# The SwiGLU down product of a hybrid decoder step as 15 rounds in place of 18 block products

## The chip, the cores and the metric

One core of one Trainium2 chip. The metric is the device time of one execution in microseconds (us), the median of several runs. All data is fp32.

## The reference

One inference step of a two-layer decoder: an mLSTM layer and then a forgetting-attention layer, each followed by a SwiGLU feed-forward block. Two request groups, a prompt of 1024 tokens (with 16 meta tokens ahead of it) and 64 sampled tokens, go through the same weights, so the feed-forward blocks work on 1104 columns of tokens. Cut to what the change touches:

```python
D_MODEL = 1024
D_FF = 2816                      # 22 tiles of 128

def swiglu(xn, w_gu, w_d):
    gu = xn @ w_gu
    return (jax.nn.silu(gu[..., :D_FF]) * gu[..., D_FF:]) @ w_d

def run_trunk(h, ...):
    for l in range(DEPTH):       # DEPTH = 2
        ...                      # mixer of the layer, added to h
        h = h + swiglu(rmsnorm(h, prm['norm_ffn'][l]), prm['w_gate_up'][l], prm['w_down'][l])
        if l == N_A_LAYERS - 1:
            shared = shared_kv(h, ...)
    y = rmsnorm(h, prm['norm_final'])
```

The change concerns the last product, `(...) @ w_d`, here called the down product: a weight of 2816 x 1024 against a hidden activation h of 2816 x 1104 (features by tokens).

## The kernel before, in words

**Layout.** Activations lie feature by token: 128 features on the partitions, tokens along the free axis. The tokens are cut into three groups `t` of 336, 384 and 384 columns (`TS`, `size`, `SL` = 384). The residual stream is in three tiles `H[t]` of eight feature tiles each (named `vA` in layer 0 and `Ht` in layer 1), with a copy `hD` in DRAM. Every fp32 product is made as three fp32r matmuls: each operand is split in a high part (a cast on ScalarE, line 338) and a low part (a subtraction on VectorE, line 339), and high x high, high x low and low x high are added in PSUM (`mm3`, lines 264 to 268).

**Feed-forward block** (`ffn`, from line 1454). First the gate and up products, in units of one feature tile (`Unit`, line 1484, matmuls on line 1505), which already use a scheme with fewer block products; the results, the tiles of h, are stored to DRAM as `hT[t]`. The last unit's leftover products are in `tail`. Then the down product.

**Down product before** (lines 1596 to 1853). `seq` is a list of 66 steps: three token groups `t`, two halves `z` of the output columns (512 each), eleven pairs `c` of h's tiles. A step multiplies two row tiles of the weight (256 x 512, one load of 512 KB, `w_load`) with two tiles of h: 4 output tiles x 2 x 3 = 24 matmuls into four PSUM banks `acc[m]`. After the eleven steps of a `(t, z)` the banks are added to `H[t]` (`add`, line 1480). With h's tiles cut in three groups this is 18 block products. h is loaded from `hT` by GpSimd's queue (`h_load`, line 1612), two tiles at a time, and split when `z` is 0; for `z` = 1 the split parts of the same group are used again. Weights are loaded five steps ahead and split two steps ahead (`w_split`). The squares for the next norm are made by `each` (`add_sq`, line 401), the norm of a finished group by `after` (layer 0, `norm_x`) or the final norm and output rows by `end` (layer 1, `final`), a little per step.

**Order.** `manual_schedule` fixes the order of the named engines to the order in which the program issues instructions; in the down stage these are TensorE, VectorE and ScalarE, while GpSimd's and SyncE's orders are chosen by the scheduler. Elsewhere (the value and key projections of `phase_a` and `phase_b`) other sets of engines are fixed, or none. Tiles that share memory wait for each other through semaphores.

**Queues.** SyncE's queue carries nearly all weights and the stores of h; GpSimd's queue carries stores of intermediate results to DRAM (`qkD`, `kD`, `qD`, `hD`, value rows) and loads of h and of some intermediate results; ScalarE issues almost no DMA.

## Time and profile before

| | |
|---|---|
| runs | 2864.53, 2862.03, 2862.07 us; median 2862.07 |
| span of the profiled execution | 2855.2 us, first to last instruction; its own time is not listed apart, the median is 6.9 us above the span |
| mean granted TensorE clock | 0.998 |
| down stage of layer 0 | 1005.0 to 1271.4 us |
| down stage of layer 1 | 2572.1 to 2844.6 us |
| DMA, whole span | 400 MB, 140 GB/s on average |

The span is the time from the first to the last instruction. The stages were read from TensorE's time line: line 266 to 268 writing the tile `dps` is the down product. A stretch's row gives the busy time of TensorE (PE), its weight loads (PEld), VectorE (DVE), ScalarE (ACT) and GpSimd (POOL), each with the number of instructions, then the granted TensorE clock, the share of the 16 DMA engines' time and GB/s. SP is SyncE. A group's row gives the line, engine and operation, what it writes and reads, the count, busy us and mean ns of one, and after the bar the idle time of the engine before these instructions with what ended it.

### The profile page before, as it was taken

What the parts mean: (1) busy time and instruction counts of PE and PEld (TensorE: products, weight loads), DVE (VectorE), ACT (ScalarE), POOL (GpSimd) and SP (SyncE); (2) the same over time, 40 slices, a digit from 0 to 9 for tenths busy, and PEclk for the clock granted to TensorE, in tenths of its full rate; (3) what the DMA queues carried; (4) which work ended last, traced back from release to release, by engine and by line L of the source; (5) the groups of instructions that cost most, each with busy time, mean ns of one, the idle gap of its engine ahead of it and who ended that gap; (6) DMA issues with size and microseconds to landing.
All of it is one profiled execution on the core that took longest, in us unless ns stands there. A gap on an engine that the chain in (4) does not pass through costs nothing.

```text
span 2855.2 us, 53625 instructions
## 1 busy us (share of the span) xinstructions
PE 2790.4 (98%) x20485; PEld 2671.0 (94%) x20485; DVE 1724.8 (60%) x3478; ACT 1311.8 (46%) x2622; POOL 1018.3 (36%) x1495
## 2 busy tenths in 40 slices
PE   7999999999999999999999999999999999999999
PEld 7998989999999999999999888777999999999999
DVE  6044555887787755553355443777478777765553
ACT  6132464444444434443344544878244444443432
POOL 3022333075556311115352202554307656531210
PEclk9999999999999999999999999999999999999999
DMA  7057655132222275544443676442412222237652
GB/s 214 19 145 175 165 160 180 48 91 76 79 84 78 95 269 198 205 144 133 149 165 129 243 282 222 156 141 87 161 60 87 79 74 84 74 102 251 221 186 99
DMA packets 312444, 400.19 MB, mean 140 GB/s; under 512 B 28143, under 2 KB 235051, under 8 KB 311163
## 3 DMA queue, kind: packets, MB, share of 16 engines
q1 hardware_dynamic: 277234, 277.79, 30.7%
q0 software_dynamic: 33728, 118.38, 12.7%
q8 instruction: 161, 2.64, 0.4%
q10 hardware_dynamic: 1224, 0.60, 0.1%
q14 instruction: 97, 0.79, 0.1%
HBM read 299.92 MB, written 96.77 MB: 139 GB/s over the span
## 4 chain that ended last, share of the span: by engine, by line
PE 71%; DVE 9%; issue 4%; ACT 3%; DMA 2%; POOL 1%; DVEq 0%; ACTq 0%; SPq 0%; POOLq 0%
PE m L1505 24%; PE dps L266 6%; PE dps L268 6%; PE dps L267 6%; PE tmps L266 3%; PE tmps L268 3%; PE tmps L267 3%; PE sp L2597 2%; DVE slot L339 2%; PE pops L268 1%; PE pops L266 1%; PE pops L267 1%; PE op L2693 1%; PE bps L266 1%; DVE s L2606 1%
## 5 line engine op out<-in xcount | busy, mean ns | idle before, releaser
L339 DVE TENSOR_TENSOR slot<-slot,slot 128x1024 fp32r<-128x1024 f32 (+3 forms) x263 | 266.4, 1015 | 129.9 <-ACT slot L338 123.6
L338 ACT CAST slot<-slot 128x1024 fp32r<-128x1024 f32 (+3 forms) x263 | 206.8, 788 | 229.3 <-PE dps L267 91.3
L1505 PE MATMUL m<-x1h,slot 128*128 128x384 f32 x640 | 178.0, 338 | 2.4 <-DVE vA L1480 0.8
L1505 PE MATMUL m<-x0h,slot 128*128 128x336 f32 x640 | 167.0, 316 | 0.0
L413 POOL TENSOR_TENSOR ns<-ns,nq 128x384 f32<-128x384 f32 (+1 forms) x59 | 63.9, 1083 | 208.8 <-ACT nq L411 207.6
L1505 PE MATMUL m<-x2h,slot 128*128 128x384 f32 x480 | 135.8, 337 | 0.0
L1612 POOL DMA_DIRECT2D hr<-hT x60 | 32.6, 543 | 283.1 <-DVE T_2l L339 69.6
L108 POOL TENSOR_TENSOR slot<-Ht 128x256 f32<-128x256 f32 x80 | 74.9, 946 | 151.3 <-DMA Ht<-in_w_gate_up 147.0
L108 POOL TENSOR_TENSOR slot<-vA 128x256 f32<-128x256 f32 x80 | 74.2, 937 | 151.5 <-DMA vA<-in_w_gate_up 147.8
L339 DVE TENSOR_TENSOR slot<-Ht,slot 128x256 fp32r<-128x256 f32 (+3 forms) x101 | 84.8, 841 | 63.7 <-ACT slot L338 63.7
L339 DVE TENSOR_TENSOR slot<-vA,slot 128x256 fp32r<-128x256 f32 (+3 forms) x101 | 85.7, 850 | 61.7 <-ACT slot L338 61.7
L1505 PEld LDWEIGHTS m<-x1h,slot 128*128 128x128 f32 x640 | 117.1, 188 | 3.4 <-DVE vA L1480 1.2
L1505 PEld LDWEIGHTS m<-x0h,slot 128*128 128x128 f32 x640 | 113.3, 188 | 0.0
L1505 PE MATMUL m<-x1l,slot 128*128 128x384 f32 x320 | 107.8, 337 | 0.0
L1505 PE MATMUL m<-x0l,slot 128*128 128x336 f32 x320 | 101.0, 316 | 0.0
L1505 PE MATMUL m<-T_2h,slot 128*128 128x384 f32 x320 | 97.1, 344 | 3.0 <-ACT Ht L1511 0.9
L2629 ACT ACTIVATE s<-s,nb 128x272 f32<-128x272 f32 (+7 forms) x126 | 98.9, 787 | 0.2 <-POOL nb L2620 0.2
L1505 PE MATMUL m<-T_4h,slot 128*128 128x384 f32 x320 | 95.9, 340 | 0.0
L2664 ACT COPY th<-tp 128x768 f32<-128x768 f32 (+1 forms) x80 | 73.6, 921 | 46.4 <-PE tp L2656 25.9
L108 POOL TENSOR_TENSOR Ht<-Ht 128x512 f32<-128x512 f32 (+1 forms) x60 | 84.5, 1409 | 28.4 <-DVE wl1l L339 28.4
L108 POOL TENSOR_TENSOR vA<-vA 128x512 f32<-128x512 f32 (+1 forms) x60 | 84.5, 1409 | 27.5 <-DVE wl0l L339 27.5
L2029 DVE TENSOR_REDUCE ss<-sqb 128x4 f32<-128x256 f32 (+1 forms) x72 | 30.2, 419 | 101.3 <-ACT sqb L2028 100.4
(838 smaller groups left out, 10267.7 us busy)
## 6 DMA issues: line engine op xcount, KB each, us to landing
slot<-in_w_down SPq DMA_DIRECT2D x88, 512.0 KB, 4.4
wr<-in_w_down SPq DMA_DIRECT2D x42, 512.0 KB, 4.5
wraw<-in_w_in_a SPq DMA_DIRECT2D x40, 512.0 KB, 4.0
vA<-in_w_gate_up SPq DMA_DIRECT2D x40, 512.0 KB, 4.0
Ht<-in_w_gate_up SPq DMA_DIRECT2D x40, 512.0 KB, 4.1
hr<-hT POOLq DMA_DIRECT2D x46, 384.0 KB, 5.2
kp<-in_cache_k SPq DMA_DIRECT2D x32, 512.0 KB, 6.2
vp<-in_cache_v SPq DMA_DIRECT2D x32, 512.0 KB, 7.4
```

The costliest lines, as they stand in the source:

```text
L108: self.net.nc.gpsimd.tensor_tensor(out=o, in0=a, in1=b, op=op)
L266: mm(ps, sh, mh, start=first, stop=False)
L267: mm(ps, sh, ml, start=False, stop=False)
L268: mm(ps, sl, mh, start=False, stop=last)
L338: self.nc.scalar.copy(hi, src)
L339: self.nc.vector.tensor_tensor(out=lo, in0=src, in1=hi.bitcast(F32), op=ALU.subtract)
L413: (nc.vector if x >= late else nc.gpsimd).tensor_tensor(out=s, in0=s, in1=sq, op=ALU.add)
L1505: nc.tensor.matmul(u.b[b][:, :n], w[p][:, k], x[q][:, k], start=new and k == i == 0, stop=k == 1 and i == 2, skip_group_check=True)
L1612: nc.gpsimd.dma_start(hraw[j], hT[t][:, 2 * c : 2 * c + 2])
L2597: nc.tensor.matmul(ps[z][:, :n], a[r, qs], b[r, at : at + n], start=(y == 0), stop=(y == 2))
L2629: nc.scalar.activation(ss[z, u], ss[z, u], AF.Exp, bias=nb[:, z : z + 1], accum_out=sm[:, u, z : z + 1])
L2664: nc.scalar.copy(th.rearrange("p x z (u h q) -> p h (x z u) q", h=2, q=64)[:, :, :n], pt[:, :, :n])
```

## The change

**The scheme.** The weight is cut in 2 column halves x 3 groups of seven row tiles (blocks `(z, k)`), h in 3 groups of seven tiles x 3 token groups (blocks `(k, t)`), which makes 18 block products. A bilinear scheme with 15 products computes the same: each round `p` multiplies a sum or difference of weight blocks with a sum or difference of blocks of h (`TERMS`), and its result, with signs, belongs to one or several of the six outputs. The 22nd tile of h and of the weight is left out of the scheme and added to some rounds as an extra row tile (round 0 is such a tile alone). Rounds are chained in PSUM: `DOWN` says for each round its sign, which outputs `(z, t)` take the running sum with which sign when the round is done, and whether the next round starts a new sum.

**Weight sums.** Four rounds use plain weight blocks (`RAW`), two a difference that GpSimd makes from two loaded blocks (`SOURCE`, `w_sub`), nine a sum that lies ready in DRAM (`COMBINED`, tiles `comb`). These are made by `combine`: a copy within DRAM issued by ScalarE and an accumulating DMA issued by GpSimd for each, in six portions that `phase_a` issues for layer 0 (during the input and the value and query/key products) and `phase_b` for layer 1 (during the value and key/query products).

**Sums of h.** Blocks of h are loaded whole from `hT` (`h_run`) and stay on chip; GpSimd forms the sums for two tiles at a time four steps ahead (`x_sum`), and each step's sum is split on ScalarE and VectorE (`x_split`) two steps ahead. Late in the stage two blocks are overwritten with sums (`merge`).

**Steps.** 62 steps of one or two row tiles. Each round boundary adds or subtracts the banks to `H` (`evict`). The norms and squares follow as the groups are finished, in another order.

**Memory and order.** The buffers of the gate and up products and the weight slots (`cg`, `cw`) are freed at the start of the stage and a new pool takes their place; in layer 0 the slots are made anew after the stage. GpSimd and SyncE are now in program order in the last unit and in the stage, too.

```diff
+RAW = {1: (0, 0), 3: (0, 2), 5: (1, 0), 6: (1, 1)}
+SOURCE = {4: ((0, 1), (0, 2)), 15: ((1, 1), (1, 2))}
+COMBINED = ((2, (0, 0), (0, 1)), (11, (0, 2), (1, 2)), (12, (1, 0), (1, 2)), (7, (0, 1), (1, 1)), (9, (0, 2), (1, 1)),
+            (8, 2, (1, 1)), (13, 11, (1, 0)), (10, 8, (1, 0)), (14, 13, (0, 0)))
+TERMS = {1: (((0, 0), 1), ((0, 1), 1), ((1, 0), -1)), 2: (((1, 0), 1),), 3: (((1, 1), 1), ((2, 0), 1), ((2, 1), 1)),
...
+DOWN = ((12, 1, ((1, 0, 1), (1, 1, -1)), None, True), (14, 1, ((0, 1, 1),), None, False),
+        (1, -1, ((0, 0, -1),), (0, 0), False),
...
+        (4, 1, ((0, 2, 1),), None, True), (0, 1, ((0, 1, 1),), (0, 1), False),
+        (9, 1, ((0, 2, 1), (1, 1, 1)), None, True),
+        (15, 1, ((1, 1, -1),), None, True), (0, -1, ((1, 2, -1),), (1, 2), False),
+        (6, 1, ((1, 2, 1),), None, True), (7, -1, ((0, 2, -1),), (0, 2), False))
...
+        for p, s, ev, last, new in DOWN:
+            js = list(range(7)) if p else []
+            if last:
+                js.append(NF - 1)
+            parts = [js[:1]] * (len(js) % 2) + [js[x : x + 2] for x in range(len(js) % 2, len(js), 2)]
+            for x, ts in enumerate(parts):
+                n = size[0] if p in (1, 5) or p in (2, 12) and x else SL
+                steps.append((p, s, ts, last, n, new and x == 0, ev if x == len(parts) - 1 else None))
...
+        def w_sub(i):
+            if i in wother:
+                n = len(steps[i][2])
+                a, b = (t[:, :n] for t in (wraw[i], wother[i]))
+                nc.gpsimd.tensor_tensor(out=a, in0=a, in1=b, op=ALU.subtract)
+                place["raw"].append(wother.pop(i))
...
+            h_run((2, 0), fresh[0], 0, 1)
+            w_load(nc.gpsimd)
+            w_load(nc.gpsimd)
+            h_run((2, 0), None, 1, 3)
+            w_load(nc.gpsimd)
+            h_run((2, 0), None, 3, 6)
+            h_run((0, 1), long(x0[1]))
+            h_run((0, 0), long(x0[0]))
+            for y in range(2):
+                w_split(y)
+                x_split(y)
+            w_load()
+            w_load()
+            for _ in tail:
+                pass
+            h_run((2, 0), None, 6, 7)
+            h_load(0, 4, 8)
+            h_load(1, 4, 8)
+            h_run((1, 0), long(x2[0]))
...
+            def evict(ev):
+                for m in range(4):
+                    for z, t, f in ev:
+                        h = H[t][:, 4 * z + m]
+                        tt(out=h, in0=h, in1=acc[m][:, : size[t]], op=ALU.add if f > 0 else ALU.subtract)
...
+            for i, (p, s, ts, last, n, lead, ev) in enumerate(steps):
+                w, x = wpart[i], xpart[i]
                 for m in range(4):
                     if lead:
                         acc[m] = bank("dps", "d")
+                    for k in range(len(ts)):
+                        for q, (a, b) in enumerate(((0, 0), (0, 1), (1, 0))):
+                            c = SL if lead and k == q == 0 else n
+                            nc.tensor.matmul(acc[m][:, :c], w[a][:, k, m * P : m * P + P], x[b][:, k, :c],
+                                             start=lead and k == q == 0, stop=k == len(ts) - 1 and q == 2,
+                                             skip_group_check=True)
...
+                if ev and (len(ts) == 1 or i == len(steps) - 1):
+                    evict(ev)
+                x_split(i + 2)
                 w_split(i + 2)
+                x_sum(i + 4)
+                w_sub(i + 3)
+                while len(wraw) <= i + 5 and w_load():
+                    pass
+                if ev and len(ts) == 2 and i < len(steps) - 1:
+                    evict(ev)
...
+def combine(self, l):
+
+    nc, w = self.nc, self.I["w_down"][l]
+    comb = self.comb[l] = {}
+    for part in (COMBINED[:5], COMBINED[5:7], COMBINED[7:]):
+        for p, a, _ in part:
+            comb[p] = self.dram.tile([7 * P, 512], F32, name=f"wc{l}_{p}")
+            nc.scalar.dma_start(comb[p], half(w, *a) if isinstance(a, tuple) else comb[a])
+        yield
+        for p, _, b in part:
+            nc.gpsimd.dma_start(comb[p], half(w, *b), accum_op=ALU.add)
+        yield
```

A step's raw weights go into three buffers, and a step of rounds 4 and 15 takes two of them. The three loads ahead of the stage are on GpSimd's queue, all later weights on SyncE's. In layer 0's `phase_a` the six portions are issued at the sixth input tile, ahead of the second and third value products, and at the 5th, 10th and 15th of the query/key products; in `phase_b` ahead of the second value product and of the first, second, fourth, fifth and seventh of the eight key/query products.

More of the change, by code (lines that the diff above doesn't have):

```diff
@@ L834, in phase_a @@
                     next(prep, None)
+                if x in (4, 9, 14):
+                    next(sums, None)
         def og_evict(m, t, ps):
@@ L1453, in ffn @@
 @_add(Net)
-def ffn(self, H, flat, l, weights, order, mix, small, each, after, end, early=None):
+def ffn(self, H, flat, l, weights, order, mix, each, after, end, cw, cb=None, early=None):
     nc, I = self.nc, self.I
@@ L1801, in ffn @@
[L1801 to L1816 removed]
+            tail = u.tail()
@@ L1848, in ffn @@
+                for _ in range(2 if p in (6, 7) else 1):
+                    next(norms, None)
+                for _ in range(99 if i == len(steps) - 1 else 2):
+                    if pend:
+                        pend.pop(0)()
             if after:
-                end(fp, pp, after(2))
+                end(dp, pp, after(2))
             else:
```

327 lines of the change are left out of this document (194 added, 133 removed), and 7 rows, old and new, of tables (DOWN, TERMS).

## The prediction

> **What bounds the kernel now.** I read the page's busy shares first, then a table of stretches over the two Down stages, then the time line of TensorE inside them, and last the other engines and the DMA queues in the places where the change puts work.
>
> ```profile
> PE 2790.4 (98%) x20485; PEld 2671.0 (94%) x20485; DVE 1724.8 (60%) x3478; ACT 1311.8 (46%) x2622; POOL 1018.3 (36%) x1495
> 1005.00:1085.00 80.00, 80.00 (x519) 80.00 (x519) 37.71 (x41) 30.88 (x36) 11.78 (x16) 1.00 0.74 252
> 1178.00:1266.00 88.00, 88.00 (x505) 87.73 (x504) 52.74 (x66) 36.58 (x53) 10.51 (x15) 1.00 0.53 181
> 2575.00:2842.00 267.00, 267.00 (x1612) 266.77 (x1611) 128.18 (x134) 97.59 (x116) 35.30 (x45) 1.00 0.57 192
> ```
>
> The last three rows are stretches inside the Down stages: their length, then the busy time of TensorE, its weight loads, VectorE, ScalarE and GpSimd, then granted clock, DMA share and GB/s. TensorE is busy for the whole of each at clock 1.00. So here a matmul less is time less, as long as nothing new makes TensorE wait; the other engines work half the stage or less.
>
> **Price of a matmul.** Rows of TensorE's time line, 336 columns wide and then 384:
>
> ```profile
> 1005.00 0.31 PE L266 MATMUL dps<-x0h,slot 128*128 128x336 f32 x1
> ...
> 1013.48 0.32 PE L267 MATMUL dps<-x0l,slot 128*128 128x336 f32 x1
> 1269.00 0.33 PE L267 MATMUL dps<-T_1l,slot 128*128 128x384 f32 x1
> ...
> 1271.27 0.33 PE L268 MATMUL dps<-T_1h,slot 128*128 128x384 f32 x1
> ```
>
> The 0.31 to 0.33 us are latencies of pipelined matmuls; the price is the distance of starts. 55 steps in 8.48 us are 0.154 us at 336 columns; 13 in 2.27 us are 0.175 at 384 (0.174 over 56 others).
>
> **The matmuls.** Before: 66 steps of 24, 1584 a layer: 528 of 336 columns (81.3 us) and 1056 of 384 (183.7 us), 265.0 us. After, counted from the list of rounds: 105 row tiles of products (15 x 7) and 6 for the last tile of h, each 4 x 3 matmuls, 1332: 336 of 336 columns (51.7 us) and 996 of 384 (173.3 us), 225.0 us. That is 40.0 us a layer, **80 us in all**. A full step (two row tiles) stays 24 matmuls, 4.17 us.
>
> **The engines beside it.** Rows of the stage of layer 0, mean in ns last before the bar, and two GpSimd rows of other stages:
>
> ```profile
> L339 DVE TENSOR_TENSOR slot<-slot,slot 128x1024 fp32r<-128x1024 f32 x40 | 49.3, 1237 | 56.6 <-ACT slot L338 56.6
> L339 DVE TENSOR_TENSOR x2l<-hr,x2h 128x768 fp32r<-128x768 f32 x8 | 7.6, 952 | 0.2 <-ACT x2h L338 0.2
> L1480 DVE TENSOR_TENSOR vA<-vA,dps 128x384 f32<-128x384 f32 x12 | 6.7, 555 | 16.8 <-PE dps L268 16.8
> L338 ACT CAST slot<-slot 128x1024 fp32r<-128x1024 f32 x40 | 41.9, 1050 | 53.9 <-DMA slot<-in_w_down 30.6 <-PE dps L267 23.1
> L338 ACT CAST x2h<-hr 128x768 fp32r<-128x768 f32 x8 | 6.7, 833 | 0.8 <-DMA hr<-hT 0.6
> L108 POOL TENSOR_TENSOR vA<-vA 128x512 f32<-128x512 f32 x40 | 57.4, 1436 | 27.5 <-DVE wl0l L339 27.5
> L2056 POOL TENSOR_TENSOR raw<-raw,gk 128x768 f32<-128x768 f32 x12 | 22.8, 1903 | 42.1 <-PE btp L2040 26.7 <-ACT sqb L2028 15.2
> ```
>
> VectorE: 55.5 weight splits of 1.24 us, as many splits of h of 0.95 (before, h was split for one half of the columns only), 76 evictions of 0.55 in place of 24 (more, because each round goes to one or two sums and the chain goes on in the same bank), and about 20 us of norms as before: some 183 of 225 us. ScalarE: 55.5 x (1.05 + 0.83) and norms, about 130. GpSimd, new: 52 sums of h of 1.90 at most, 8 merges, differences of weights in two rounds (the two rows give 1.82 us more per 1000 columns, so 2.37 for 1024): 130 to 150 with its DMA issues. A three-term round asks 3.8 us of GpSimd per 4.17 us step. All fit, so I price them at nothing; TensorE covers them, and with two steps of lookahead a late one shows only if it stays late. Banks: eviction follows each quarter step, so a round that evicts to one place holds nothing up. Two rounds evict to two places just before a short step: 1.1 us a quarter against 0.52 of matmul, about 2 us each.
>
> **The new chain in rounds 4 and 15.** Their weights are a difference of two halves, loaded as a pair into three raw buffers. A step's second half can be loaded only when the subtraction before has freed its buffer.
>
> ```profile
> slot<-in_w_down SPq DMA_DIRECT2D x88, 512.0 KB, 4.4
> vA<-in_w_gate_up SPq DMA_DIRECT2D x40, 512.0 KB, 4.0
> vA<-hD POOLq DMA_DIRECT2D x4, 1536.0 KB, 9.5
> qk<-qkD POOLq DMA_DIRECT2D x8, 512.0 KB, 7.1
> q1 hardware_dynamic: 277234, 277.79, 30.7%
> q0 software_dynamic: 33728, 118.38, 12.7%
> ```
>
> Load 4.0 to 4.4 us and subtraction 2.4 make 6.4 to 6.8 us per step against 4.17, three times in a row, with one to two steps ahead as cover: followed step by step with the split (1.05 + 1.24) behind it, round 4 loses 2.3 to 3.4 us and round 15, behind two short steps and the double eviction, 4.5 to 5.4. Ends 0 (loads landing in 3 us) and 9 a layer; I take 7, **+14**, by the 4.0 row, since no h is being loaded by then.
>
> **Start of the stage.** h is no longer streamed: 4.9 MB of h and weights and 1.4 MB of residual go through GpSimd's queue at once, issued in order from about 7 us before the stage, as the last unit's tiles come free. q0's bytes over its share (118.38 MB in 12.7% of 2855 us) are 326 GB/s, q1's 317. Tile 20 of h lands about 10 us into the stage and the residual about 16; step 3 wants the first 8 us in, the first eviction wants the second at 13, and the next step waits for that eviction since the chain stays in its bank. Behind that wait on VectorE stand the splits two steps on. Ends 0 (before, the hand-over shows no gap) and 9 (1.5 MB landing alone in 9.5 us); I take 5 a layer, **+10**.
>
> A TensorE wait may cost more than itself:
>
> ```profile
> 218.32 0.21 PE L1214 MATMUL n0p<-ident,n 32*128 32x32 f32 x1 [1.51 <-DMA n<-in_state_n]
> 217.00:219.00 2.00, 0.68 (x11) 0.67 (x13) 0.21 (x1) 0.00 (x0) 0.29 (x1) 1.00 1.15 249
> 219.00:221.00 2.00, 2.00 (x19) 1.83 (x14) 0.00 (x0) 0.00 (x0) 0.00 (x0) 0.83 1.23 183
> 221.00:223.00 2.00, 2.00 (x8) 2.00 (x7) 0.00 (x0) 0.00 (x0) 0.00 (x0) 0.50 1.19 295
> ```
>
> After a wait of 1.5 us the granted clock is 0.83 and then 0.50 for 4 us in all, 1.3 us of work lost. It followed small matmuls, not dense ones, so I add nothing for it. The Trainium skill, TensorE: Matmul & The Clock Gate, section "HAM oscillation", puts the point at gaps above about 3.4 us; by that rule only the stage's first waits could matter, some 1.7 us each, an estimate, and the sum would be about 2820; the trace's drop came after a shorter gap, so no run here supports the threshold itself.
>
> **Hand-over to the next phase.** Layer 0's weight slots are now freed and made anew after the stage, on top of buffers that the first value products still use. The first loads and splits of the next projection may come late by a 4.1 us load; ends 0 and 8, **+3**. The tail (the last evictions, squares and rows out) keeps its form: 0, ends -2 and 2.
>
> **The sums of weights in DRAM.** A layer has 9 copies (issued by ScalarE) and 9 accumulations (GpSimd) of 1.835 MB. Issue costs 0.4 to 0.9 us each on idle parts of their engines. The transfers share the 16 DMA engines with all loads, and the accumulations stand in GpSimd's queue ahead of its stores and loads; ScalarE must wait for an accumulation before some copies, with its evictions behind that wait.
>
> ```profile
> 65.00:137.00 72.00, 72.00 (x622) 72.00 (x621) 4.90 (x4) 13.58 (x30) 0.00 (x0) 1.00 0.12 27
> 137.00:200.00 63.00, 60.19 (x375) 58.22 (x374) 30.32 (x61) 20.57 (x33) 14.35 (x26) 1.00 0.44 134
> 200.00:235.00 35.00, 31.09 (x203) 29.62 (x203) 10.28 (x24) 8.40 (x14) 15.74 (x25) 0.95 0.95 197
> 1380.00:1408.00 28.00, 28.00 (x246) 28.00 (x246) 13.07 (x30) 12.84 (x35) 10.33 (x15) 1.00 0.44 145
> 1395.77 0.61 POOL L2049 DMA_DIRECT2D kDh<-bhi  x1
> 1404.57 0.61 POOL L2049 DMA_DIRECT2D kDh<-bhi  x1
> ```
>
> Layer 0's first five lie beside 65 to 137 us, where DMA is at 0.12: free. Its last two accumulations fall near 200, where DMA is at 0.95 and the recurrence's loads (7.1 us each) use the same queue. Layer 1's lie beside 27 us projections at 0.3 to 0.5. No row shows a copy within DRAM or an accumulation: from q0's rate 5.6 us each (9 x 5.6 = 51 us a layer, hidden), three times that (17 us) if reading twice and writing once cost in turn. Ends 0 and 80; I take **+8**, near the low end, because the stretches are mostly half idle. The Trainium skill, DMA: Bandwidth & Descriptors, section "Anatomy of one DMA", gives 2.0 us plus bytes over 436,000 per us for this queue, which would make 6.2 us each, an estimate; it says nothing of accumulation there, and the sum stays.
>
> **Sum.** -80 + 14 + 10 + 3 + 8 = -45 against the profiled execution, whose span is 2855.2 us, 6.9 under the median of 2862.07 that I carry it to: **2817 us**.
>
> **Rivals.** (1) All cover holds: the waits shrink to a few us and the time is 2782 to 2797. For it: half-idle engines and DMA shares of 0.53 to 0.74. Against it: the load-subtract chain is longer than a step. (2) Slower, by one mechanism: the accumulations hold up GpSimd's queue. If one takes 17 us, layer 1's five are 85 us of queue, and the stores of kD, a pair each 9 us (the two rows above) from two buffers, wait behind them; ScalarE stops for a free buffer and TensorE behind it. Some 20 us for that part, 25 for each of the two later ones and 30 for layer 0's last: 100 in place of 8, 2909 us. It decides when the total passes 53 us, at about 11 us an accumulation. Against it: the first five have a whole projection before kD's first store. (3) VectorE becomes the bound: 183 of 225 us is 81%, and in the rounds with a norm a step asks 0.95 + 1.24 + 0.55 + 1.1 of 4.17. One step in three late by 1 us is 20 a layer: 2857. Against it: its waits today are for ScalarE, not on itself.
>
> **How the numbers follow.** Forecast 0.50 (2797 to 2840), all covered 0.25, VectorE 0.14 (2840 to 2862), slower 0.11. Three runs spread over 2.5 us, so 0.2% (5.7 us) is about what can be told from no change. Faster 0.50 + 0.25 + 0.12, same 0.02, slower 0.11. The range goes from the floor with every wait gone, 2784, to 2860.
>
> **What would show it.** Right: 1332 matmuls a Down stage in 230 to 245 us; TensorE waits for VectorE at the fourth and fifth step; ScalarE waits for GpSimd's subtraction in rounds 4 and 15; phases before unchanged within 8 us. Wrong: stages of 225 us (1), kD's stores landing late with ScalarE waiting for them (2), TensorE waiting for splits in most steps (3), or matmuls whose distance is no longer 0.174 us.

## The result, and the profile after

The changed kernel takes 3190.31 us (3187.41 to 3193.6, four runs) beside 2862.66 us for the kernel before (2862.03 to 2864.53). The ratio is 1.1147, with a 95% interval of 1.1131 to 1.1163. The prediction was 2817 us.

The page of the changed kernel, busy shares of the span and a few rows of the span in 40 slices of 79.7 us:

```profile
span 3188.7 us, 53051 instructions
PE 2776.9 (87%) x19981; PEld 2636.7 (83%) x19981; DVE 1905.4 (60%) x3647; ACT 1321.2 (41%) x2670; POOL 1291.6 (41%) x1602
PE   0222999989999999887899999999999999999987
PEclk9965999999999999998999999999999999999989
DMA  9999257563222222843444438654242222218443
```

TensorE has 504 matmul instructions less, as meant (20485 to 19981), and is busy 14 us less, but for 87% of a longer span, not 98%. Two places show in its row. In the first four slices, 0 to 319 us, it is nearly idle and the DMA row stands at 9: nothing of the change was meant to be there. And in the two Down stages (slices 16 to 19 and 36 to 39) 7s and 8s now stand, in the first stage throughout and in the second in its later half, where before the row had 9 throughout.

Stretches of the kernel before, then of the changed one (length, busy time of TensorE, its weight loads, VectorE, ScalarE and GpSimd, granted clock, DMA share, GB/s): the first 330 us, the Down stage of layer 0, and the 40 us behind it.

```profile
0.00:330.00 330.00, 305.85 (x2196) 289.33 (x2197) 146.08 (x350) 115.63 (x256) 80.15 (x151) 0.99 0.54 143
1005.00:1270.00 265.00, 265.00 (x1581) 264.55 (x1581) 144.34 (x174) 109.33 (x145) 35.92 (x50) 1.00 0.60 204
1271.00:1311.00 40.00, 39.78 (x330) 39.18 (x329) 17.65 (x29) 13.99 (x35) 27.11 (x107) 1.00 0.58 194
```

```profile
0.00:330.00 330.00, 70.22 (x410) 66.03 (x411) 42.89 (x120) 41.87 (x94) 47.73 (x82) 0.79 1.00 244
1270.00:1565.00 295.00, 248.91 (x1344) 238.96 (x1343) 235.09 (x244) 114.89 (x163) 166.45 (x92) 0.93 0.53 179
1564.00:1604.00 40.00, 29.74 (x223) 28.31 (x221) 18.62 (x30) 12.28 (x27) 21.93 (x99) 0.89 0.47 156
```

The difference of the two spans is 333.5 us. From the starts of the first and the last matmul of each Down stage:

| part | before | after | difference |
|---|---|---|---|
| up to the first Down matmul | 1005.0 | 1269.9 | +264.9 |
| Down stage, layer 0 | 266.3 | 294.1 | +27.8 |
| between the stages | 1300.8 | 1321.0 | +20.2 |
| Down stage, layer 1 | 272.4 | 291.6 | +19.2 |
| tail | 10.7 | 12.1 | +1.4 |

So there are two losses. Both Down stages got longer, though each has 252 matmuls less, and most of the loss lies in the first 330 us, long before the first of them.

**The first 330 us.** What ScalarE and TensorE waited for there in the changed kernel (us in all, times, longest):

```profile
ACT x2h L757 <- DMA wc<-in_w_down: 78.3, 2, 64.7
ACT x0h L757 <- DMA wc<-in_w_down: 75.7, 2, 54.4
ACT rb L722 <- DMA wc<-in_w_down: 25.0, 1, 25.0
PE hps L741 <- ACT hs L758: 169.4, 6, 62.2
```

`wc` are the sums of weights in DRAM. ScalarE's casts of x stand in its queue behind copies of `wc` that wait for an accumulation, and TensorE waits for those casts. The copies from w_down and the accumulations, summed up by line (duration of the issuing instruction in ns min/median/max, first and last start in us):

```profile
L2008 ACTq DMA_DIRECT2D wc<-in_w_down x10: 503/4234/17396, 5.5 to 184.9; - x10
L2011 POOL DMA_DIRECT2D wc<-in_w_down x18: 1202/1220/1439, 19.7 to 310.7; - x18
```

All ten copies from w_down, layer 1's too, are issued between 5.5 and 185 us, and all 18 accumulations between 20 and 311 us. The program writes layer 1's beside the cache phase, some 1500 us later. The order of these instructions is the scheduler's: nothing that the program computes has to be done before the copies. An issue also took up to 17.4 us of ScalarE itself.

**The Down stage.** Groups of VectorE's instructions in layer 0's stage of the changed kernel (busy us, mean ns, idle before):

```profile
L361 DVE TENSOR_TENSOR dn0wl<-dn0raw,dn0wh 128x1024 fp32r<-128x1024 f32 x48 | 79.8, 1662 | 9.9 <-ACT dn0wh L360 9.2
L361 DVE TENSOR_TENSOR dn0xl<-dn0tmp,dn0xh 128x768 fp32r<-128x768 f32 x13 | 18.3, 1408 | 7.9 <-ACT dn0xh L360 7.9
L1939 DVE TENSOR_TENSOR vA<-vA,dps 128x384 f32<-128x384 f32 x52 | 25.4, 546 | 0.0
```

The split of 1024 columns took 1237 ns before and takes 1662; that of 768 columns 952 and now 1408. The eviction is as it was, 555 and 546. A stretch of VectorE's time line beside GpSimd's shows what decides:

```profile
1416.36 1.21 DVE L361 TENSOR_TENSOR dn0wl<-dn0raw,dn0wh 128x1024 fp32r<-128x1024 f32 x1
1417.49 2.59 DVE L361 TENSOR_TENSOR dn0xl<-dn0tmp,dn0xh 128x768 fp32r<-128x768 f32 x1
1420.01 2.86 DVE L361 TENSOR_TENSOR dn0wl<-dn0raw,dn0wh 128x1024 fp32r<-128x1024 f32 x1
1426.40 1.94 DVE L1939 TENSOR_TENSOR vA<-vA,dps 128x384 f32<-128x384 f32 x4
```

```profile
1415.14 0.90 POOL L665 DMA_DIRECT2D hD<-vA  x1
1416.52 2.75 POOL L1694 TENSOR_TENSOR dn0tmp<-hr,x0l 128x768 f32<-128x768 f32 x1 [0.48 <-DVE dn0xl L1713]
1419.35 2.44 POOL L1694 TENSOR_TENSOR dn0tmp<-dn0tmp,x1l 128x768 f32<-128x768 f32 x1
```

The split that starts in GpSimd's pause (1416.36) takes 1.21 us; the next ones, beside a sum of h, take 2.59 and 2.86, and the sum itself 2.75 in place of 1.90. Over the whole stage, the 18 splits of 1024 columns that lie beside no arithmetic of GpSimd take 1.22 us on average, and the 30 others 1.93. The eviction reads one operand in SBUF and one in PSUM and is not touched: 545 ns beside GpSimd's arithmetic and 546 without it. TensorE's waits in the stage, and one of them with the clock behind it:

```profile
PE dps L1957 <- DVE vA L1939: 29.1, 9, 6.9
PE dps L1957 <- DVE dn0wl L361: 9.1, 10, 2.3
PE dps L1957 <- ACT dn0wh L360: 5.8, 2, 4.7
1502.21 0.66 PE L1957 MATMUL dps<-dn0xh,dn0wh 128*128 128x384 f32 x1 [6.93 <-DVE vA L1939]
1504.00:1506.00 2.00, 2.00 (x8) 2.00 (x7) 1.86 (x3) 0.92 (x1) 2.00 (x2) 0.50 0.03 9
1508.00:1510.00 2.00, 2.00 (x13) 2.00 (x12) 0.68 (x1) 0.00 (x0) 0.88 (x1) 1.00 0.78 250
```

The 294 us are 225 of matmuls, 46 in which TensorE is idle, and the rest a slower clock: 0.93 over the stage, because it stands at 0.50 for some 3 to 6 us after most of the waits above 2 us.

### The profile page after: what moved, and what is told of

It reads as the page before. It is cut to its first block, busy times and chain, and to the rows that moved or that the text cites. A ratio compares the mean times of both kernels' runs of the same rounds, so it can differ in the third digit from the quotient of the medians.

```text
span 3188.7 us, 53051 instructions
## 1 busy us (share of the span) xinstructions
PE 2776.9 (87%) x19981; PEld 2636.7 (83%) x19981; DVE 1905.4 (60%) x3647; ACT 1321.2 (41%) x2670; POOL 1291.6 (41%) x1602
## 4 chain that ended last, share of the span: by engine, by line
PE 52%; DVE 13%; issue 6%; DMA 5%; ACT 4%; POOL 3%; ACTq 0%; DVEq 0%; SPq 0%; POOLq 0%
PE m L1536 20%; PE dps L1957 5%; PE tmps L287 3%; PE tmps L288 3%; PE tmps L286 3%; PE sp L2761 2%; PE op L2857 1%; DVE dn0wl L361 1%; DVE slot L361 1%; PE pops L286 1%; PE pops L287 1%; PE pops L288 1%; DVE dn1wl L361 1%; PE bps L286 1%; POOL dn1tmp L1694 1%
## 5 line engine op out<-in xcount | busy, mean ns | idle before, releaser
L1957 PE MATMUL dps<-dn0xh,dn0wh 128*128 128x384 f32 (+1 forms) x444 | 155.3, 350 | 36.1 <-DVE vA L1939 29.1
L1957 PE MATMUL dps<-dn1xh,dn1wh 128*128 128x384 f32 (+1 forms) x444 | 154.3, 347 | 26.3 <-DVE Ht L1939 20.1
L361 DVE TENSOR_TENSOR slot<-slot,slot 128x512 fp32r<-128x512 f32 (+3 forms) x175 | 155.0, 887 | 24.1 <-ACT slot L360 17.7
L1957 PE MATMUL dps<-dn0xh,dn0wl 128*128 128x384 f32 (+1 forms) x444 | 153.6, 346 | 9.1 <-DVE dn0wl L361 9.1
L1957 PE MATMUL dps<-dn1xh,dn1wl 128*128 128x384 f32 (+1 forms) x444 | 152.5, 344 | 4.8 <-DVE dn1wl L361 4.8
L1957 PE MATMUL dps<-dn0xl,dn0wh 128*128 128x384 f32 (+1 forms) x444 | 152.7, 344 | 0.9 <-DVE dn0xl L361 0.9
L1957 PE MATMUL dps<-dn1xl,dn1wh 128*128 128x384 f32 (+1 forms) x444 | 152.1, 343 | 0.6 <-DVE dn1xl L361 0.6
L360 ACT CAST slot<-slot 128x512 fp32r<-128x512 f32 (+3 forms) x175 | 114.5, 657 | 78.5 <-PE m L1536 67.5
L1957 PEld LDWEIGHTS dps<-dn0xh,dn0wh 128*128 128x128 f32 x444 | 88.3, 199 | 41.5 <-issue 28.8
L1957 PEld LDWEIGHTS dps<-dn1xh,dn1wh 128*128 128x128 f32 x444 | 87.9, 198 | 30.6 <-issue 18.3
## 6 DMA issues: line engine op xcount, KB each, us to landing
wc<-in_w_down POOLq DMA_DIRECT2D x18, 1792.0 KB, 34.2
```

Source lines behind the costliest of these rows:

```text
L360: self.nc.scalar.copy(hi, src)
L361: self.nc.vector.tensor_tensor(out=lo, in0=src, in1=hi.bitcast(F32), op=ALU.subtract)
L1957: nc.tensor.matmul(acc[m][:, :c], w[a][:, k, m * P : m * P + P], x[b][:, k, :c], start=lead and k == q == 0, stop=k == len(ts) - 1 and q == 2,
```

## The experiments

All are the changed kernel with the edit shown. Ratios are against the kernel before, run on the same chip. The experiments ran on several chips, on which the kernel before took 2861 to 2864 us, so differences of a few us between experiments are read from the ratios.

### e1: no sums of weights

```
-   nc.scalar.dma_start(comb[p], half(w, *a) ...)
-   nc.gpsimd.dma_start(comb[p], half(w, *b), accum_op=ALU.add)
-   get(w, 0, 0, js[0], len(js), 0, self.comb[l][p])
+   get(w, 0, 0, js[0], len(js))
```

> Leaves out the sums of weights in DRAM: no copies, no accumulations; the nine rounds that read a sum read the top left part of w_down in its place, the same bytes. Theory: the changed kernel lost its time in two places that have nothing to do with each other, some 265 us in the first 330 us of the span, where the copies and accumulations of both layers now stand, and some 55 us in the two Down stages. Then this kernel takes 2915 to 2935 us, the first 1000 us look as before the change, and the Down stages stay at about 300 and 290 us. Rival: the early loss comes from something else that the change moved (pools, order of loads): then about 3190 us again. Second rival: the stages are long because the loads of summed weights come late: then the stages shrink as well, to about 230 us each, and the time is near 2800 us.

2930.45 us, ratio 1.0233 (1.0215 to 1.0251). The first matmul of the first Down stage is at 1007.5 us, and the stages are 294.9 and 293.2 us long. The two losses are separate: 260 us for the sums, some 69 for the rest.

### e2: sums at the place where the program writes them

```
+   self.tc.keep_in_program_order(        # behind the instruction written before it on its engine
        nc.scalar.dma_start(comb[p], ...))
+   self.tc.keep_in_program_order(nc.gpsimd.dma_start(comb[p], half(w, *b), accum_op=ALU.add))
```

> All sums made, but each copy and accumulation is held in its engine's order behind the instruction written before it, so that they run where the program has them (layer 0: first projections, layer 1: projections of the cache phase). Theory: the loss of 265 us was the place and not the transfers; 10 to 40 us remain, for ScalarE's waits before the dependent copies and for DMA traffic: 2930 to 2970 us. Rival: the transfers cost their time wherever they stand (18 accumulations of 15 to 30 us each in GpSimd's queue): over 3050 us.

3110.6 us, ratio 1.0868 (1.0844 to 1.0893). The rival's side: only 80 of the 260 us come back. The DMA queues of this kernel (packets, MB, share of 16 engines):

```profile
q0 software_dynamic: 48768, 152.11, 17.4%
q10 hardware_dynamic: 10728, 33.64, 3.3%
```

The same without sums (e1):

```profile
q0 software_dynamic: 32352, 119.08, 12.2%
q10 hardware_dynamic: 1224, 0.60, 0.1%
```

The spans are 3108.1 and 2930.7 us. So the 18 accumulations take 183 us of all 16 engines, 10.2 us each, and the copies 5.5 each: 141 us a layer. At the written places that meets a DMA that is already half in use: the first 330 us of this kernel have a DMA share of 0.79 and 228 us of TensorE work in place of 304 in e1. The first Down matmul comes at 1105.5 us, 98 later than in e1. Layer 1's places cost nearly as much, 79 us more between the stages than in e1: there GpSimd's queue waits 40 us in all for accumulations ahead of other transfers, and ScalarE waits 32.9 us for the stores of kD, for which it does not wait at all in e1.

### e3: copies issued by GpSimd

```
-   nc.scalar.dma_start(comb[p], ...)
+   nc.gpsimd.dma_start(comb[p], ...)
```

> Copies issued by GpSimd in place of ScalarE, everything else as in the changed kernel: the order again puts them all early, but ScalarE's queue holds none. Theory: the loss at the start is ScalarE standing in order behind copies that it could not issue yet; without them most of 265 us comes back: 2930 to 3000 us. Rival: it is the DMA traffic, or GpSimd's queue with the stores and low parts behind the accumulations: 3100 us or more.

3172.38 us, ratio 1.1089 (1.106 to 1.1117): the rival again. ScalarE's queue holds no copy, yet nearly all of the loss stays. The first 330 us, and ScalarE's longest wait in them:

```profile
0.00:330.00 330.00, 96.80 (x586) 91.14 (x587) 50.63 (x125) 49.63 (x107) 59.42 (x100) 0.67 1.02 249
ACT hs L758 <- DMA hD<-hs: 148.5, 7, 28.5
```

The DMA engines are full (1.02). The start needs trips of blocks of x through DRAM (`hD`); their stores, which GpSimd issues, land 16 to 52 us after issue (median 40; 4.5 in e1), and ScalarE waits up to 28.5 us at a time. GpSimd itself waits 231 us in these 330 for transfers of the sums. The rival named DMA traffic and GpSimd's queue; this run does not part them, and whether the same wait would stand behind ScalarE's in the changed kernel is not shown.

### e5: sums in the gate and up stage

```
+   sums = self.combine(l)            # one copy or accumulation per next(), kept in program order
    for x in range(3, NF - 1):        # the 18 units of the gate and up stage
        ...
+           if g == 2:
+               next(sums)
```

> All sums of weights made, each layer's 9 copies and 9 accumulations one at a time, one per unit of the layer's own gate and up stage, in an order in which each finds its source long done. By the queue rows of the kernel with the sums at their written places, an accumulation takes 10.2 us of all 16 DMA engines and a copy 5.5, 141 us a layer; the gate and up stage has 450 us with a DMA share of 0.25. Theory: the sums cost what they take from a busy DMA and from queues behind them; here both are free, so the time is that of the kernel without sums plus 0 to 15 us: 2930 to 2945 us. Rival: ScalarE's issue of a copy (5 to 14 us in the two runs before) and GpSimd's issue stop the engines in any place: 18 x 5 us or more a layer on ScalarE, beyond 2980 us.

2931.22 us, ratio 1.0229 (1.0212 to 1.0246): as without sums, 259 us under the changed kernel. The stretch of 500 us ahead of the Down stage in the kernel before and here, and the copies:

```profile
500.00:1000.00 500.00, 494.20 (x2877) 488.90 (x2876) 391.42 (x590) 236.99 (x468) 251.26 (x248) 1.00 0.25 79
500.00:1000.00 500.00, 494.04 (x2874) 488.08 (x2873) 391.08 (x585) 235.71 (x466) 261.88 (x257) 1.00 0.53 141
L2007 ACTq DMA_DIRECT2D wc<-in_w_down x10: 497/507/592, 634.4 to 2578.4; - x10
```

The DMA share there goes from 0.25 to 0.53 and TensorE stays at 494 us. With one transfer on its way at a time an issue takes 0.51 us, not up to 17.4. The sums cost the DMA as much as in e2, but here they cost no time. This kernel does the whole computation and is what the change would have been with another place for its sums.

### e4 and e8: less of GpSimd's work

```
    # e4, on e1                                        # e8, on e4
-   if js and len(TERMS[p]) == 1 and len(js) == len(ts):    -   src = SOURCE.get(p)
+   if js and len(js) == len(ts):                           +   src = None
        return
```

> As the kernel without sums of weights, and GpSimd's sums of h are left out too: rounds of two and three terms split their first term alone (only the few steps with a row of the last tile of h keep theirs, with the merges and the differences of weights). VectorE's and ScalarE's work and all matmuls stay. Theory: the stages are long because VectorE's splits and GpSimd's sums slow each other: a weight split falls from 1.66 to under 1.35 us, the stages to 235 to 250 us, the time to 2800 to 2830 us. Rival: VectorE is late by its own load (evictions and splits in one queue): a split is still 1.6 us or the stages stay over 280 us, 2900 us or more. Between, some 2860 us: both.

> As the kernel without sums of weights and without GpSimd's sums of h, and rounds 4 and 15 load one half of w_down in place of two and leave out the difference. Theory: of the 54 us that the stage still is above its matmuls there, the load-and-subtract chain of rounds 4 and 15 carries 10 to 20 (four waits of 2 to 6 us around them), so 20 to 40 us less in all: 2870 to 2890 us. Rival (the term of the prediction, 7 us a layer, taken as an upper end with the cover of two steps): 2893 to 2905 us.

2907.7 us (1.0158, 1.0141 to 1.0175) and 2884.87 us (1.0075, 1.0058 to 1.0091). The splits fall to 1343 ns in e4, as expected, but the stages only to 282.6 and 278.9 us and the time to the rival's 2900 or more: the sums of h are 23 us of the loss, not 100. Each step showed something behind it. With GpSimd free sooner its loads of h and of the residual start sooner too, the burst of loads at the start of the stage gets denser (from 1035 to 1045 us the DMA share is 1.01, in e1 0.58), a weight load of round 1 comes late in it, and TensorE's wait there grows from 1.7 to 8.4 us (named after the eviction, which stands behind the split of that weight). e8 takes off another 23 us, in the range that the theory gave.

### e6: evictions ahead of the splits

```
-   if ev and (len(ts) == 1 or i == len(steps) - 1):
+   if ev:
        evict(ev)
    x_split(i + 2); w_split(i + 2); ...
-   if ev and len(ts) == 2 and i < len(steps) - 1:
-       evict(ev)
```

> The kernel without sums of weights, with one change in VectorE's order: at the end of every round the four evictions stand ahead of the splits for the step after the next, in place of behind them. Theory: the waits of 4 to 7 us at round ends (some 35 of the 48 us that TensorE waits in layer 0's Down stage) are evictions that stand behind a split which itself waits for a late sum of h; with the order turned most of them go, a part comes back as waits for splits before one-row steps: stages 270 to 280 us, 2885 to 2905 us in all. Rival: VectorE simply has too much to do, and the order moves the wait from one name to another: stages within 5 us of 296 and 293, 2920 to 2940 us, with TensorE's waits now for the splits.

2938.42 us, ratio 1.0259 (1.0242 to 1.0276). TensorE's waits in the stage of layer 0:

```profile
PE dps L1957 <- DVE dn0wl L361: 17.1, 15, 2.3
PE dps L1957 <- ACT dn0wh L360: 8.8, 6, 5.0
PE dps L1957 <- DVE vA L1939: 2.3, 3, 1.6
```

The wait for evictions falls from 29 to 2.3 us, and the others grow. The rival holds, though the stage of layer 1 grew by 6 us, to 299.6, where it had asked for at most 5: the name in the list of waits was that of the last in a late queue.

### e7: sums of h on VectorE

```
-   nc.gpsimd.tensor_tensor(out=o, in0=a, in1=runs[r][:, j, :n], ...)
+   nc.vector.tensor_tensor(out=o, in0=a, in1=runs[r][:, j, :n], ...)
```

> The kernel without sums of weights, with all 52 sums of h a layer made by VectorE in place of GpSimd. VectorE gets some 50 us more by its own durations (0.95 us for 768 columns). Theory: a GpSimd sum costs VectorE about as much as it saves (splits 1.66 instead of 1.24 us while both run), so that the move changes little: splits fall to 1.3 us, VectorE's busy time in the stage stays within 15 us, the time within 15 us of 2930. Rival: the two engines do not disturb each other and splits are long for another reason: VectorE's busy time grows by the full 50 us and the stage to over 320 us, 2980 us or more.

2940.64 us, ratio 1.0265 (1.0248 to 1.0282): by the ratios 9 us over e1, inside the theory's 15. Stretches of 280 us in the stage, without sums first and then with VectorE making the sums of h:

```profile
1010.00:1290.00 280.00, 234.76 (x1263) 224.83 (x1263) 222.04 (x226) 108.86 (x150) 160.74 (x90) 0.93 0.55 184
```

```profile
1010.00:1290.00 280.00, 230.70 (x1247) 222.67 (x1246) 217.95 (x277) 105.00 (x144) 53.02 (x37) 0.93 0.55 187
```

VectorE has 51 instructions more and is busy 4 us less, while GpSimd loses 108 us of work. By its price beside a quiet GpSimd (0.95 us) the 52 sums would have been some 50 us more. So a sum on GpSimd cost VectorE about all that it would have taken there itself.

### e9: the high part read from PSUM

On e5, two PSUM banks that stand free in the Down stage take a second copy of the high part:

```
+   nc.scalar.copy(hi[:, :n], wraw[i][:, :n])
+   for k in range(n):
+       b = bank("hp", "f")
+       nc.scalar.copy(b, hi[:, k].bitcast(F32))
+       tt(out=lo[:, k], in0=wraw[i][:, k], in1=b, op=ALU.subtract)
```

> The whole computation, with the sums of weights in the gate and up stage, and one change: ScalarE writes the high part of each weight piece a second time, into two PSUM banks that stand free in the Down stage, and VectorE takes the low part as SBUF piece minus PSUM piece, 512 columns at a time, so that it reads one SBUF operand and not two. Theory (the two engines disturb each other where both read two SBUF operands; evictions with one SBUF and one PSUM operand kept 546 ns all along): a 512-column split takes 0.65 to 0.7 us also while GpSimd works, GpSimd's 768-column sums fall from about 2.5 to about 2.0 us, the stages get 5 to 15 us shorter each, 2900 to 2920 us. Rival: the slowing does not depend on where the operands lie: two 512-column splits still take 1.7 us together, and ScalarE's extra 1.2 us a step make it 2930 to 2950 us.

2904.86 us, ratio 1.0139 (1.0122 to 1.0155), 26 us under e5, with no work left out. VectorE's splits and one of GpSimd's sums in the stage of layer 0:

```profile
L1678 DVE TENSOR_TENSOR dn0wl<-dn0raw,hp 128x512 fp32r<-128x512 f32 x108 | 69.7, 681 | 31.9 <-ACT hp L1677 31.0 <-issue 1.0
L1692 POOL TENSOR_TENSOR dn0tmp<-hr,x2l 128x768 f32<-128x768 f32 x3 | 5.5, 1842 | 6.8 <-DVE dn0xl L361 6.8
```

A split of 1024 columns, now two pieces, takes 2 x 681 ns beside a working GpSimd. The 108 pieces take 665 to 691 ns, though 65 of them lie beside arithmetic of GpSimd. This sum goes from 2762 ns in e5 to 1842; it moved the most, and the 27 sums of 768 columns go from 2391 to 1975 on average. Besides the place of one operand, the edit halves the split and gives ScalarE a second write. The halving is not what helps: in e10, beside a quiet GpSimd, a split of 512 columns from SBUF takes 690 ns and one of 1024 takes 1223. The Trainium skill, SBUF — State Buffer, section "Who interferes with whom", says that VectorE with two SBUF inputs contends with a GpSimd instruction that reads SBUF, and with at most one, outside its two-port modes, does not. By that rule the splits of h, left as they were, should stay slow: the trace agrees (13 of 768 columns at 1173 ns, 10 at 1392; the 20 beside arithmetic of GpSimd 1480 on average, the 15 others 946).

### e10 to e13: what is left

Each on e8. e10: squares on VectorE, no merges. e11: only the last eviction into each place. e12: both. e13: e12 without the residual's load.

```
    # e10                                       # e11
-   self.add_sq(H, t, m, sp, x, 4)              +   if gone.get((z, t), 0) + 1 < ...:   # not the last
+   self.add_sq(H, t, m, sp, x, 0)              +       continue
-   if p in (4, 9, 0) and merge and i > 40:         # e13
+   if False:                                   -   nc.gpsimd.dma_start(H[t][:, a:b], self.hD[...])
```

> As the kernel without sums of weights, sums of h and weight differences, and now GpSimd has next to no arithmetic in the Down stages: the sums of squares go to VectorE, the merges of runs are left out. Theory (what is left of the 47 us above the matmuls is still the two engines disturbing each other): splits at 1.24 us, stage of layer 0 under 260 us, 2855 to 2870 us. Rival (what is left is the burst of loads at the start and VectorE's own chain of evictions and splits): 2875 to 2890 us.

> As the kernel without sums of weights, sums of h and weight differences, with the evictions of a round left out unless they are the last into their place: 24 a layer as before the change, in place of 76; TensorE then goes from round to round without a wait for VectorE. Theory (evictions in the middle of a chain are what the rounds add to TensorE's path): some 15 us less a layer, from the waits named for evictions (8.6 us for the residual's load, and 1 to 3 us at five round ends), 2850 to 2860 us. Rival (splits and loads set the pace, the evictions only show where): 2875 to 2885 us.

> Both of the two before together: no arithmetic of GpSimd and 24 evictions a layer. If the causes named so far are all, the stage is its matmuls plus the burst of loads at the start (225 + 10 us), and the time 2835 to 2850 us, 10 to 25 us under the kernel before the change: the 20 us of the hand-over after layer 0 stay. Rival: a cause not named yet holds the stages at 250 us or more, 2865 us or more.

> As the kernel without GpSimd arithmetic and with 24 evictions a layer, and the residual (2 x 4.4 MB from DRAM, issued in the first 70 us of each stage) is not loaded: the evictions add to what stands in its place. Theory (the 28 us a layer that the stage there still is above its matmuls come mostly from the burst of h, residual and weights in its first 55 us, where the DMA share is 1.0 and the weight loads come late): 5 to 12 us less a layer, 2828 to 2842 us. Rival (the start is latency of the chain load, high part, low part, and not bytes): within 4 us of 2851.

e10 2864.93 us (1.0003, 0.9993 to 1.0012); e11 2859.32 (0.9985, 0.9975 to 0.9995); e12 2850.97 (0.9955, 0.9938 to 0.9972); e13 2834.94 (0.9902, 0.9885 to 0.9918). In e10 the split is at 1223 ns, its old price, and the stage of layer 0 at 262 us, a little over the theory's 260. e12 lies a little above the theory's band and keeps stages of 253 and 254 us, which the rival had asked for; e13 says what part of that is. Two stretches of 10 us, some 30 us into the stage, in e12 and then in e13:

```profile
1040.00:1050.00 10.00, 7.64 (x43) 6.73 (x41) 3.28 (x4) 3.42 (x4) 2.29 (x3) 1.00 1.03 397
1050.00:1060.00 10.00, 6.62 (x32) 6.07 (x33) 2.70 (x3) 1.71 (x2) 0.00 (x0) 0.85 1.02 418
```

```profile
1040.00:1050.00 10.00, 10.00 (x59) 10.00 (x59) 4.32 (x5) 3.94 (x5) 0.00 (x0) 1.00 1.02 420
1050.00:1060.00 10.00, 9.32 (x59) 8.87 (x58) 5.59 (x7) 4.36 (x5) 0.00 (x0) 1.00 0.69 261
```

With fewer bytes the burst at the start ends some 10 us sooner, the weights are there and TensorE is nearly full; the stages are 242 and 244 us. The first begins 4.3 us later, though, the part between them grows by 2.4, and the whole gain is 16 us. So of the 28 us above the matmuls, about 8 are bytes. What the rest is, the first chain of load, high part and low part or small waits, no run parts.

### e14 and e15: the work moved rather than left out

e14 is e9 with the squares on VectorE. e15 is e14 with the differences for rounds 4 and 15 made in the gate and up stage:

```
+   keep(nc.sync.dma_start(t[z], part(half(w, *b), z)))
+   keep(nc.scalar.activation(t[z], t[z], AF.Copy, scale=-1.0))
+   keep(nc.gpsimd.dma_start(part(d, z), t[z]))
    ...                                     # after the seven row tiles
+   keep(nc.gpsimd.dma_start(d, half(w, *a), accum_op=ALU.add))
```

> The whole computation: sums of weights in the gate and up stage, splits with the high part in PSUM, and the sums of squares in the Down stages on VectorE in place of GpSimd (18 additions a layer, 1.4 us on GpSimd, 0.56 on VectorE). Theory (GpSimd is the longer queue, its three-term sums are what the splits wait for): 5 to 12 us less than with the split from PSUM alone, 2893 to 2900 us. Rival (VectorE's own queue is what counts): 2903 to 2912 us.

> As the one with the squares on VectorE, and the differences of weights for rounds 4 and 15 are made in the gate and up stage too: ScalarE negates one half, 128 rows at a time, it is stored to DRAM and the other half accumulated onto it; rounds 4 and 15 then load one piece like the others. Theory (the load-and-subtract chain costs 11 us a layer, as the kernel without it showed): 18 to 26 us less, 2868 to 2880 us, still above the kernel before the change. Rival (what those rounds waited for was VectorE's backlog, or the extra work disturbs the gate and up stage): less than 8 us gained, 2888 us or more.

2901.94 us (1.0144, 1.0127 to 1.0161) and 2896.87 us (1.0119, 1.0102 to 1.0136). Both theories asked for more. By its ratio e14 gains nothing over e9 (1.0139), and e15 is 5 us under e14, as its rival had it. In e15 the stages fall from 277.1 and 277.8 to 268.0 and 262.5 us, the 24 us that the theory gave. But the first Down matmul comes 8.8 us later and the part between the stages grows by 12.8: most of what the load-and-subtract chain cost is paid again in the gate and up stage, where TensorE now waits for ScalarE's evictions. Ahead of the first Down stage of e15:

```profile
PE m L1529 <- ACT vA L1535: 9.1, 9, 5.3
```

In e14 that row is 1.6 us. e15 is the fastest changed kernel that does the whole computation, and it is still 1.2% above the kernel before; e12, which leaves out all this work, is only 0.45% below it. No version here that does the whole computation wins.

## Why the prediction was wrong, point by point

- **Matmuls, -80 us: right.** 1332 a layer (3 x 444 by line and tile), at 0.174 us where TensorE does not wait.
- **DRAM sums, +8 (ends 0 to 80): the step that failed, by 251 us.** Measured 259 (3190 against 2931 in e5). Two errors are in it. I took the sums to run where the program writes them, and the trace shows all of them issued in the first 311 us; that is worth 80 us (e2). And I priced an accumulation at 5.6 us, "hidden"; it takes 10.2 us of the whole DMA and the copy that I left out 5.5, so a layer needs 141 us of DMA and not 51. Between 65 and 137 us, where I had put five of nine, there was room for 63. The upper end of 80 was also too low for the written places, 180 us (e2 against e1). The issue price of 0.4 to 0.9 us held for ScalarE's copies only with one on its way (0.51 in e5); in the changed kernel the median is 4.2.
- **Other engines at nothing: the second step that failed.** I added up VectorE at 183 of 225 us by durations measured beside a quiet GpSimd (36 us of work in 265) and put 130 to 150 us on GpSimd beside it. The stage shows VectorE at 235 us and GpSimd at 166 of 295. The two prices were right each by itself and wrong together: in e10, with GpSimd at 17 us, VectorE is at 182, the forecast's figure.
- **A clock term of 0: wrong.** I added nothing, since the one drop in the trace of before followed small matmuls. Here the clock was 0.93 over the stage, some 20 us of 295. The Trainium skill, TensorE: Matmul & The Clock Gate, section "HAM oscillation", puts its point at gaps above 3.4 us, and that was nearer than my 0: in layer 0's stage a drop followed each of the five waits above 3.4 us. It is not borne out as a limit: in e9 a wait of 2.33 us was followed by matmuls at 0.50 for 3 us.
- **Rounds 4 and 15, +14:** 23 us when left out (e8), and 24 in the Down stages when moved (e15). The mechanism was right: ScalarE waits 20.8 us in layer 0's stage for the subtraction, the sign that was asked for. The size was too small, 7 a layer where leaving the chain out gives 11 to 12; why is not shown, since e8 takes away the second load as well as GpSimd's work.
- **Start of the stage, +10:** the place was right: waits of 4.7 and 1.7 us and a slow clock behind the first in layer 0. The first is the one forecast, though the list names the weights: ScalarE's cast of the last tiles of h waits 9.3 us for their load, which ends 13 us into the stage and not 10, and the cast of the weights stands behind it. No wait for the residual is seen there: the first evictions go straight after a split, and at the second wait VectorE goes without a pause from a split, slow beside GpSimd, to the eviction. Its bytes counted all the same once other work was gone: leaving its load out gave 16 us over both layers (e13).
- **Hand-over, +3:** measured 20.2. TensorE waits 5.9 us for the last norm and then 4.4 and 3.0 for the first weights in the remade slots; 29.74 us of work in 40 after the stage, at clock 0.89. I had priced one late load, and neither the norm nor the clock. VectorE's load in the stage is not the reason: e13, where it is busy 160 of 243 us, has the same 5.9.
- **Rivals.** The second (accumulations too dear, deciding at about 11 us each) named the right transfer. One takes 10.2 us of the DMA and lands 23.8 us after issue in e2, and its mechanism, GpSimd's queue held up and ScalarE waiting for the stores of kD, is seen there, at the written places. It had 100 us in all, where e2 shows 180, and nothing of the changed kernel's own order. The third (VectorE becomes the bound) named the right engine for the stage, at 20 us a layer where 70 stood above the matmuls. The first has its form in e12 and e13: with nearly all added work gone the time is 2851 and 2835, not 2782 to 2797. None had both losses at once.
- **What would show it.** The stages were to take 230 to 245 us; they take 294 and 292. The phases ahead were to stay within 8 us and grew by 265. Of the signs against the forecast "TensorE waiting for splits in most steps" came nearest: e6 shows 21 waits for the weights' splits in 62 steps, once the evictions are out of their way.

The two stages and the hand-over together are 67 us of loss for 80 us of matmuls saved: 147 us of new waits and slower clock. Left out one after another, sums of h give 23, differences 23, squares and merges 20, evictions 14 (26 without the step before), the residual's load 16. How much of that is the two engines in each other's way and how much is VectorE's own work is shown only in part: 26 us for the weight splits (e9). The splits of h were not tried with an operand in PSUM.

## What to carry to other kernels

An instruction that depends on nothing has no place in the program until something holds it there: look up where the scheduler puts it before pricing what covers it, and then price its DMA time against the idle DMA of that stretch, in engine time and not in latency. Shares of VectorE and GpSimd could not be laid side by side here, where both read two operands in SBUF: count a GpSimd sum as if VectorE made it (e7), or give VectorE one operand in PSUM (e9). And where TensorE is full, a wait can cost more than itself: the 46 us of waits in layer 0's stage came with some 20 us of clock.

## What the runs showed of the hardware that I had not expected

- An accumulation of 1.835 MB within DRAM takes 10.2 us of all 16 DMA engines, 1.9 times a copy of the same size (5.5), and lands 15.8 us after issue (median) with one sum on its way at a time (e5), 34.2 in the changed kernel.
- Issuing a copy of 896 rows of 2 KB held ScalarE 0.5 us when it was alone and up to 17.4 us with others on their way.
- A split of two SBUF operands beside GpSimd took 2.59 or 2.86 us where it takes 0.95 or 1.21 alone. The times fit waiting for GpSimd's instruction rather than sharing with it: in the rows above the split from 1417.49 ends 0.81 us after GpSimd's sum, and the next one 1.08 us after the next sum. With one operand in PSUM a split of 512 columns takes 0.68 us with or without GpSimd's arithmetic beside it (e9).
- The clock fell to 0.50 also after a wait of 2.33 us, for about 3 us, but not after every such wait: one of 2.32 us in the changed kernel and one of 2.90 in e1 (at 2806.8 us) were followed by a clock of 1.00. So the length alone does not decide it. Rows of e9, the wait and two stretches behind it, and then of the changed kernel, a wait and the stretch behind it:

```profile
1180.75 0.66 PE L1958 MATMUL dps<-dn0xh,dn0wh 128*128 128x384 f32 x1 [2.33 <-DVE vA L1940]
1182.00:1184.00 2.00, 2.00 (x8) 2.00 (x7) 1.88 (x2) 0.09 (x1) 1.50 (x1) 0.50 0.50 190
1184.00:1186.00 2.00, 2.00 (x12) 2.00 (x12) 0.89 (x1) 2.00 (x3) 0.00 (x0) 0.97 0.60 128
```

```profile
1487.01 0.44 PE L1957 MATMUL dps<-dn0xh,dn0wl 128*128 128x384 f32 x1 [2.32 <-DVE dn0wl L361]
1487.00:1489.00 2.00, 1.99 (x11) 1.99 (x12) 2.00 (x3) 0.00 (x0) 1.92 (x2) 1.00 0.35 117
```
